# Unscaled token rows stored by tile for the experts' gathers, the factor in a column behind them, and x loaded by tiles

## The chip, the cores and the metric

The kernel runs as one program on one core of one Trainium2 chip. The metric is the device time of one execution, in microseconds; smaller is better. Inside the core five engines work side by side, each through its own list of instructions in a fixed order: PE (TensorE, matrix products), DVE (VectorE) and ACT (ScalarE) for elementwise work, POOL (GpSimd) for small work and for issuing some transfers, and SP (SyncE), which here only issues transfers. An instruction that waits for another engine or for a transfer holds up all that stands behind it in its own list.

## The reference, cut to what matters

The model has two layers on 512 tokens of width 1024: a mixer (differential attention in layer 0, sparse attention in layer 1), and after each a mixture of experts. For the experts each token is divided by its root mean square, scaled and shifted by two vectors, and sent to two of 32 experts:

```
h   = rmsnorm(x) * (1 + scale) + shift          # x: 512 x 1024
top = two best of 32 experts per token (4 groups of 8)
y_e = (silu(h @ w_gate[e]) * (h @ w_up[e])) @ w_down[e]      # hidden width 256
x   = x + gate2 * sum over the two experts of weight * y_e
```

## The kernel before

**Residual.** The residual rows live in the tile `xs` (128 partitions x 4 token tiles x 1024). It is filled from the input by one transfer of 2 MB that ACT issues (L644) while layer 0's output projection runs. That projection (`out_proj`) works on token tiles 0 and 1 first, then 2 and 3; the results of each half are multiplied into `otmp` (L607) and added to `xs` (L608) on DVE. Then PE transposes `xs` for the router (L700), token tile by token tile.

**Routing.** For each token tile `route` computes the router's logits (transposes L700, copies on ACT L702, products L705), then the factor 1/rms, called `r4` in the code and `r_h` in the rows (ACT square with sum L326, DVE L327, POOL power L328). The helper `row` multiplies the token rows by that factor on DVE (L728) and POOL stores the result in the DRAM buffer `xr_d` (L729). A table of slots says which tokens go to which expert, 64 slots for each expert. After the table there is a branch for experts with more tokens than slots (L949); it is not taken here.

**Experts.** The 32 experts run as 16 pairs, 128 slots a pair, numbered 0 to 15 below. For each pair, in the function `pair`: POOL gathers 128 rows of `xr_d` (L838) into one of two buffers `xg`; PE transposes them in two lots of four (L852) and ACT (L857) and DVE (L859) copy the transposes to `xT`, scaling and shifting them; PE multiplies with the gate and up weights (L864, 32 products of 128x512 to a pair of 64-column halves); ACT forms `sl` (L867), DVE forms `ac` (L869); PE transposes `ac` (L873), and a copy to `aTm` follows. That copy is made by the helper `copy_any`, which takes ACT and DVE in turn: even pairs have it on ACT (L394), odd pairs on DVE (L395). DVE makes the one-hot matrix `st` (L881), PE multiplies with the down weights (L887, first half `b_sc`, second half `b_mm`, 8 products each), and each half passes through `y` (DVE, L890), `yh` (ACT, L370) and `yl` (DVE, L371).

The function `add` of a pair brings its result back to the token rows: 8 times two products (L898 and L899 on PE) and one addition into `xs` (L900 on DVE). It is called inside the next pair, between `aTm` and `st` in program order. For PE it is work that needs nothing of the pair whose `ac` and `aTm` are under way.

**Order.** A scheduler puts every engine's instructions in a fixed order when the program is built, from the dependences and from its own estimate of times; the kernel is written in the plain order above. The same scheduler orders the changed kernel anew, with other results. Weights stream through SP in pieces of 512 KB ahead of the pairs that need them.

Of the kernel before, what the change touches and what calls it, by code (L numbers as in the profile page):

```python
# [11 lines left out]
F32 = mybir.dt.float32  # L12
# [4 lines left out]
AF = mybir.ActivationFunctionType  # L17
OP = mybir.AluOpType
# [4 lines left out]
P = 128  # L23
S = 512
NT = S // P
D = 1024
# [55 lines left out]
def tile_kernel(ctx, tc, x, c, positions, ada_w, ada_b, norm_g, final_g, diff_w_in, diff_w_out,  # L82
# [3 lines left out]
    nc = tc.nc  # L86
    mm = nc.tensor.matmul
    x_d = x.rearrange("b s d -> (b s) d")
    out_d = out.rearrange("b s d -> (b s) d")

    dram = ctx.enter_context(tc.tile_pool(name="dram", bufs=1, space=DRAM))
# [6 lines left out]
    def bank(tag):  # L98
        return ps.tile([P, 512], F32, name="b_" + tag, tag=tag, bufs={"mm": 4, "tr": 2, "sc": 2}[tag])
# [35 lines left out]
    def slot(i, shape, dtype=F32):  # L135

        return rp.tile(shape, dtype, name=f"slot{i}", tag=f"slot{i}", bufs=1)
# [4 lines left out]
    ident = cst.tile([P, P], F32, name="ident")  # L142
# [125 lines left out]
    with tc.tile_pool(name="rope", bufs=1) as rpool:  # L268
# [3 lines left out]
        kk = rpool.tile([P, NT, 8], F32, name="kk")  # L272
# [50 lines left out]
    def rms(pool, xt, rcol, tag=("junk", 1)):  # L323

        junk = pool.tile([P, D], BF16, name="junk", tag=tag[0], bufs=tag[1])
        nc.scalar.activation(junk, xt, AF.Square, accum_out=rcol)  # L326
        nc.vector.tensor_scalar(rcol, rcol, 1.0 / D, EPS, op0=OP.mult, op1=OP.add)  # L327
        nc.gpsimd.tensor_tensor(rcol, rcol, mhalf[:, 0:1], op=OP.pow)  # L328
# [6 lines left out]
    def by_k(row):  # L335

        return row.rearrange("t (p k) -> t k p", k=KC)
# [31 lines left out]
    def stack_k(src, h_out, l_out):  # L369
        nc.scalar.activation(h_out, src, AF.Copy)  # L370
        nc.vector.tensor_tensor(l_out, src, h_out.bitcast(F32), op=OP.subtract)  # L371
# [19 lines left out]
    def copy_any(dst, src):  # L391
        ev[0] += 1
        if ev[0] % 2:
            return nc.scalar.activation(dst, src, AF.Copy)  # L394
        return nc.vector.tensor_copy(dst, src)  # L395

    class Experts:
# [47 lines left out]
        def gu(self, e, k):  # L445
            return self.have["g", e, k // 4][:, :, k % 4, :]

        def dn(self, e, k, z):
            return self.have["d", e, 0][:, k, z * 512:(z + 1) * 512]
# [191 lines left out]
    main.close()  # L641
    xpool = ctx.enter_context(tc.tile_pool(name="xs", bufs=1))
    xs = xpool.tile([P, NT, D], F32, name="xs")
    nc.scalar.dma_start(xs, x_d.rearrange("(t p) d -> p t d", p=P))  # L644


    def tap(name, xs):
        if name in TAPS:
            nc.sync.dma_start(TAPS[name].rearrange("(t p) d -> p t d", p=P), xs)

    xr_d = dram.tile([S, D], F32, name="xr_d")

    def open_moe(l):
        st = ExitStack()
# [31 lines left out]
    def open_moe2(l, g):  # L686
        g.st2 = ExitStack()
        g.mq = g.st2.enter_context(tc.tile_pool(name=f"moeb{l}", bufs=1, side="right"))
        g.xg = [g.mq.tile([P, D], F32, name=f"xg{i}") for i in range(2)]

    def apx(t, dims, off=0):
        return bass.AP(tensor=t.tensor, offset=t.offset + off, ap=[t.ap[0]] + dims)
# [1 line left out]
    def logits(g, lb, t):  # L694

        xk = by_k(g.xs[:, t, :])
        for q in range(2):
            b = bank("tr")
            for kk in range(4):
                nc.tensor.transpose(b[:, kk * P:(kk + 1) * P], xk[:, 4 * q + kk, :], ident)  # L700
            ht = g.mp.tile([P, 512], F32, name="ht", tag="xT", bufs=2)
            nc.scalar.activation(ht, b, AF.Copy)  # L702
            for kk in range(4):
                k = 4 * q + kk
                mm(lb[:, t * NL:(t + 1) * NL], ht[:, kk * P:(kk + 1) * P], g.wr[:, k, :],  # L705
                   start=(k == 0), stop=(k == KC - 1), skip_group_check=True)

    def route(l, g):
        mp, mq, xs = g.mp, g.mq, g.xs
        fold_router(g)  # L710
        lb = bank("sc")
        r4 = mp.tile([P, NT], F32, name="r_h")
# [10 lines left out]
        oh2 = oh.rearrange("p (c t) e -> p c (t e)", c=2)  # L723
        M = mq.tile([P, NT, NE], BF16, name="M")

        def row(t):
            xr = g.xg[t] if t < 2 else mq.tile([P, D], F32, name="xr", tag="yh" if t == 2 else "yl", bufs=1)
            nc.vector.tensor_scalar(xr, xs[:, t, :], r4[:, t:t + 1], None, op0=OP.mult)  # L728
            g.stored = nc.gpsimd.dma_start(xr_d[t * P:(t + 1) * P, :], xr)  # L729

        for t in range(NT):
            logits(g, lb, t)
            rms(mp, xs[:, t, :], r4[:, t:t + 1])
            if t < NT - 1:
                row(t)
        for t in range(NT):
            nc.vector.scalar_tensor_tensor(lg[:, t], lb[:, t * NL:(t + 1) * NL], r4[:, t:t + 1], g.rb, op0=OP.mult, op1=OP.add)
            nc.vector.max(g8[:, t], lg[:, t, 0:8])
# [5 lines left out]
        for t in range(NT):  # L744
# [3 lines left out]
                                       op0=OP.mult, op1=OP.add)  # L748
        nc.vector.tensor_tensor(oh, dup(g.iota[:, 0:NE], 2 * NT),
                                eid.rearrange("p c t -> p (c t)")[:, :, None].to_broadcast([P, 2 * NT, NE]), op=OP.is_equal)  # L750
        nc.vector.tensor_tensor(M.rearrange("p t e -> p (t e)"), oh2[:, 0], oh2[:, 1], op=OP.add)
        row(NT - 1)

        rk = bank("sc")
        mm(rk[:, 0:P], upper, M.rearrange("p t e -> p (t e)"), start=True, stop=False, skip_group_check=True)
# [86 lines left out]
    def pair(g, q, tab, gu, dn, xg, between=None):  # L842


        mp = g.mq
        toks, tokf, wts = tab
        xT = g.mp.tile([P, KC, P], F32, name="xT", bufs=2)
        for z in range(2):
            b = bank("tr")
            for kk in range(4):  # L850
                k = 4 * z + kk
                nc.tensor.transpose(b[:, kk * P:(kk + 1) * P], by_k(xg)[:, k, :], ident)  # L852
            for kk in range(4):
                k = 4 * z + kk
                src = b[:, kk * P:(kk + 1) * P]
                if kk % 2:
                    nc.scalar.activation(xT[:, k, :], src, AF.Identity, scale=g.Ac[:, k:k + 1], bias=g.shc[:, k:k + 1])  # L857
                else:
                    nc.vector.tensor_scalar(xT[:, k, :], src, g.Ac[:, k:k + 1], g.shc[:, k:k + 1],  # L859
                                            op0=OP.mult, op1=OP.add)  # L860
        hb = bank("mm")
        for k in range(KC):
            for a in range(2):
                mm(hb[64 * a:64 * a + 64, :].rearrange("p (z n) -> p z n", z=2), xT[:, k, 64 * a:64 * a + 64], gu(a, k),  # L864
                   start=(k == 0), stop=(k == KC - 1), skip_group_check=True)
        sl = mp.tile([P, HID], F32, name="sl", bufs=2)
        nc.scalar.activation(sl, hb[:, 0:HID], AF.Silu)  # L867
        ac = mp.tile([P, HID], F32, name="ac", bufs=2)
        nc.vector.tensor_tensor(ac.rearrange("p (k t) -> p t k", k=2), hb[:, HID:512].rearrange("p (t k) -> p t k", k=2),  # L869
                                sl.rearrange("p (t k) -> p t k", k=2), op=OP.mult)  # L870
        b = bank("tr")
        for k in range(2):
            nc.tensor.transpose(b[:, k * P:(k + 1) * P], ac[:, k * P:(k + 1) * P], ident)  # L873
        aT = mp.tile([P, 2, P], F32, name="aTm", bufs=2)
        copy_any(aT.rearrange("p k t -> p (k t)"), b[:, 0:HID])
        if between is not None:
            between()
        yh = mp.tile([P, D], F32R, name="yh", bufs=1)
        yl = mp.tile([P, D], F32R, name="yl", bufs=1)
        st = mp.tile([P, S], F32R, name="st", bufs=2)  # L880
        nc.vector.tensor_scalar(st, g.iota, tokf[:, q:q + 1], None, op0=OP.is_equal)  # L881
        for z in range(2):
            yb = bank("mm" if z else "sc")
            zz = slice(z * 512, (z + 1) * 512)
            for k in range(2):
                for a in range(2):
                    mm(yb[64 * a:64 * a + 64, :], aT[:, k, 64 * a:64 * a + 64], dn(a, k, z), start=(k == 0), stop=(k == 1),  # L887
                       skip_group_check=True)
            y = mp.tile([P, 512], F32, name="y", bufs=2)
            nc.vector.scalar_tensor_tensor(y, yb, wts[:, q:q + 1], g.g2[:, zz], op0=OP.mult, op1=OP.mult)  # L890
            stack_k(y, yh[:, zz], yl[:, zz])

        def add():
            for t in range(NT):
                for z in range(2):
                    zz = slice(z * 512, (z + 1) * 512)
                    b = bank("mm" if z else "sc")
                    mm(b, st[:, t * P:(t + 1) * P], yh[:, zz], start=True, stop=False)  # L898
                    mm(b, st[:, t * P:(t + 1) * P], yl[:, zz], start=False, stop=True)  # L899
                    nc.vector.tensor_tensor(g.xs[:, t, zz], g.xs[:, t, zz], b, op=OP.add)  # L900

        return add
# [57 lines left out]
    g = open_moe(0)  # L960
# [3 lines left out]
    wout_stack.close()  # L964
    tap("x0a", g.xs)
    open_moe2(0, g)
    experts(0, g, ew, route(0, g))
    tap("x0m", g.xs)

# [8 lines left out]
    xr = [slot(i, [P, 2, D]) for i in range(2)]  # L978
# [103 lines left out]
    b = bank("tr")  # L1082
# [44 lines left out]
    b = bank("tr")  # L1127
# [4 lines left out]
    b = bank("mm")  # L1132
# [12 lines left out]
    b = bank("mm")  # L1145
# [104 lines left out]
    g = open_moe(1)  # L1250
# [5 lines left out]
    wout_stack.close()  # L1256
    tap("x1a", g.xs)
    open_moe2(1, g)
    experts(1, g, ew, route(1, g))
    tap("x1m", g.xs)  # L1260
    fg = bcp.tile([P, D], F32, name="bc")
# [33 lines left out]
```

## Time and profile before

| | us |
|---|---|
| median of 3 runs | 1410.16 (1410.09 to 1411.47) |
| the profiled execution, its own time | 1411.33 |
| its span, first to last instruction | 1409.5 |
| PE busy | 1282.6 (91%) |
| DVE busy | 786.7 (56%) |
| ACT busy | 514.6 (37%) |
| POOL busy | 169.4 (12%) |

The span is what the trace shows; the own time of that execution is 1.8 us longer, and the median of the timed runs lies 1.2 us under that own time. Busy shares are means over the whole span. The mean clock granted to PE over the span is 0.956 of full speed.

### The profile page before, as it was taken

To read this page: it belongs to the slowest core of one execution; us is meant where nothing else is said; L and a number is where in the kernel's file an instruction comes from. 1 tells how busy PE (TensorE), PEld (TensorE's weight loads), DVE (VectorE), ACT (ScalarE), POOL (GpSimd) and SP (SyncE) were. 2 spreads that over 40 slices of the span, in tenths; PEclk is the share of its full clock that TensorE was granted. 3 is DMA by queue.
4 is the path that set the end of the run, shared out by engine and by line. 5 is a ranking of instruction groups with operands and counts; after the bars stand their busy time and mean duration, and the time that the engine had idled before them with its cause. 6 is when DMAs were issued, how large, how long until landed. Compare 5 with 4: busy or idle time off the path is not lost. (4 is left out here: it accounts for less than half of the span.)

```text
span 1409.5 us, 18225 instructions
## 1 busy us (share of the span) xinstructions
PE 1282.6 (91%) x6431; PEld 759.2 (54%) x6431; DVE 786.7 (56%) x1791; ACT 514.6 (37%) x1188; POOL 169.4 (12%) x298
## 2 busy tenths in 40 slices
PE   4899999978879999999799799999999699999995
PEld 0687668567733544444588555555568434444342
DVE  2454755485635666655554365656635446666555
ACT  2454544454322222111454444656644212222212
POOL 0021020211110000000042111111220200000000
PEclk7899999999989999999899899999999699999998
DMA  7633764585579999992332174510153599999931
GB/s 253 219 104 112 244 209 150 180 289 193 185 244 363 390 405 408 379 350 95 109 120 90 60 255 147 148 51 1 54 161 120 182 362 369 407 408 409 364 141 60
DMA packets 104493, 309.81 MB, mean 220 GB/s; under 512 B 13776, under 2 KB 27568, under 8 KB 104388
## 3 DMA queue, kind: packets, MB, share of 16 engines
q1 hardware_dynamic: 93920, 288.59, 57.4%
q0 software_dynamic: 6240, 12.95, 2.7%
q10 hardware_dynamic: 4228, 6.96, 1.6%
q8 instruction: 55, 0.90, 0.3%
q14 instruction: 50, 0.41, 0.1%
HBM read 310.51 MB, written 6.33 MB: 225 GB/s over the span
## 5 line engine op out<-in xcount | busy, mean ns | idle before, releaser
L864 PE MATMUL b_mm<-slot,xT 128*64 128x512 f32 x640 | 199.3, 604 | 0.0
L864 PE MATMUL b_mm<-ring,xT 128*64 128x512 f32 x384 | 135.9, 597 | 0.0
L362 PE MATMUL b_mm<-wh,h_hi 128*128 128x512 f32 (+1 forms) x320 | 116.1, 394 | 8.3 <-ACT wh L358 6.6
L363 PE MATMUL b_mm<-wl,h_hi 128*128 128x512 f32 (+1 forms) x320 | 122.5, 391 | 0.7 <-DVE wl L359 0.7
L364 PE MATMUL b_mm<-wh,h_lo 128*128 128x512 f32 (+1 forms) x320 | 120.6, 387 | 0.0
L857 ACT ACTIVATE xT<-b_tr,col_sh,col_A 128x128 f32<-128x128 f32 x128 | 56.5, 455 | 148.2 <-DVE xT L859 146.9
L864 PEld LDWEIGHTS b_mm<-slot,xT 128*64 128x64 f32 x640 | 58.1, 139 | 87.3 <-issue 80.6
L900 DVE TENSOR_TENSOR xs<-xs,b_sc 128x512 f32<-128x512 f32 x128 | 83.4, 683 | 23.0 <-PE b_sc L899 23.0
L900 DVE TENSOR_TENSOR xs<-xs,b_mm 128x512 f32<-128x512 f32 x128 | 82.1, 682 | 19.3 <-PE b_mm L899 19.3
L189 PE MATMUL b_mm<-ring,csil 128*32 128x512 f32 x384 | 76.0, 657 | 11.8 <-DMA ring<-in_ada_w_dram 6.9
L838 POOL DMA_INDIRECT xg<-xr_d,toks x32 | 32.0, 1000 | 432.3 <-PE b_tr L852 411.8
L867 ACT ACTIVATE sl<-b_mm 128x256 f32<-128x256 f32 x32 | 12.3, 385 | 186.9 <-PE b_mm L864 186.9
L869 DVE TENSOR_TENSOR ac<-b_mm,sl 128x256 f32<-128x256 f32 x32 | 19.7, 617 | 107.7 <-ACT sl L867 107.7
L359 DVE TENSOR_TENSOR wl<-ring,wh 128x512 fp32r<-128x512 f32 (+1 forms) x80 | 53.1, 672 | 35.9 <-ACT wh L358 34.3
L1216 ACT ACTIVATE pT<-b_tr 128x512 f32<-128x512 f32 x80 | 47.4, 597 | 65.2 <-PE b_tr L1214 64.6
L362 PEld LDWEIGHTS b_mm<-wh,h_hi 128*128 128x128 f32 x320 | 60.3, 191 | 19.9 <-ACT wh L358 7.3
L386 DVE TENSOR_REDUCE nm<-b_sc 128x1 f32<-128x128 f32 (+3 forms) x116 | 54.3, 482 | 27.5 <-PE b_sc L381 26.8
L370 ACT ACTIVATE yh<-y 128x512 fp32r<-128x512 f32 x64 | 39.9, 632 | 79.5 <-DVE y L890 79.5
L363 PEld LDWEIGHTS b_mm<-wl,h_hi 128*128 128x128 f32 x320 | 61.0, 191 | 12.4 <-DVE wl L359 1.4
L358 ACT ACTIVATE wh<-ring 128x512 fp32r<-128x512 f32 (+1 forms) x80 | 48.4, 614 | 50.7 <-PE b_mm L364 36.2
L364 PEld LDWEIGHTS b_mm<-wh,h_lo 128*128 128x128 f32 x320 | 60.8, 190 | 11.1
L864 PEld LDWEIGHTS b_mm<-ring,xT 128*64 128x64 f32 x384 | 39.9, 137 | 49.4 <-issue 46.8
(329 smaller groups left out, 2678.5 us busy)
## 6 DMA issues: line engine op xcount, KB each, us to landing
ring<-in_ada_w_dram SPq DMA_DIRECT2D x96, 512.0 KB, 4.9
slot<-in_moe_w_gate_dram SPq DMA_DIRECT2D x80, 512.0 KB, 8.4
slot<-in_moe_w_up_dram SPq DMA_DIRECT2D x80, 512.0 KB, 4.4
dn<-in_moe_w_down_dram SPq DMA_DIRECT2D x80, 512.0 KB, 8.0
slot<-in_moe_w_down_dram SPq DMA_DIRECT2D x48, 512.0 KB, 8.6
ring<-in_moe_w_gate_dram SPq DMA_DIRECT2D x48, 512.0 KB, 10.1
ring<-in_moe_w_up_dram SPq DMA_DIRECT2D x48, 512.0 KB, 4.4
ring<-in_diff_w_in_dram SPq DMA_DIRECT2D x24, 512.0 KB, 4.8
```

What stands on the lines that cost most here:

```text
L189: mm(acc[32 * g:32 * g + 32, :], lhsT, w[:, c0:c0 + 512], start=(k == 0), stop=(k == KC - 1), skip_group_check=True)
L358: nc.scalar.activation(wh[:, :n], w[:, k, :], AF.Copy)
L359: nc.vector.tensor_tensor(wl[:, :n], w[:, k, :], wh[:, :n].bitcast(F32), op=OP.subtract)
L362: mm(accs[t][:, :n], hi[:, k, tt], wh[:, :n], start=(k == 0), stop=False)
L363: mm(accs[t][:, :n], hi[:, k, tt], wl[:, :n], start=False, stop=False)
L364: mm(accs[t][:, :n], lo[:, k, tt], wh[:, :n], start=False, stop=(k == KC - 1))
L370: nc.scalar.activation(h_out, src, AF.Copy)
L386: nc.vector.tensor_reduce(nm, b[:, :n], axis=AX.X, op=OP.max, negate=True)
L857: nc.scalar.activation(xT[:, k, :], src, AF.Identity, scale=g.Ac[:, k:k + 1], bias=g.shc[:, k:k + 1])
L864: mm(hb[64 * a:64 * a + 64, :].rearrange("p (z n) -> p z n", z=2), xT[:, k, 64 * a:64 * a + 64], gu(a, k), start=(k == 0), stop=(k == KC - ...
L900: nc.vector.tensor_tensor(g.xs[:, t, zz], g.xs[:, t, zz], b, op=OP.add)
L1216: nc.scalar.activation(pT, b, AF.Copy)
```

## The change

The residual `xs` is loaded in four transfers of 512 KB, one for each token tile, in place of one. `xr_d` and the two `xg` buffers get one column more (1025). The rows of `xs` are stored in `xr_d` as they are, right behind each tile's logits, and DVE's four multiplications by the factor per layer (L728) are gone. The factors of all 512 tokens go into the last column by one more POOL transfer of 512 single numbers; the event `g.stored`, after which a stretch of weight transfers may start, is now that transfer. POOL clears both `xg` buffers once a layer. In `pair` a new ACT instruction multiplies the gathered rows by their last column into a new tile `xn` (one buffer), and the transposes read `xn`. The tile `y` has one buffer in place of two.

```diff
-    nc.scalar.dma_start(xs, x_d.rearrange("(t p) d -> p t d", p=P))
+    for t in range(NT):
+        nc.scalar.dma_start(xs[:, t, :], x_d[t * P:(t + 1) * P, :])
...
-    xr_d = dram.tile([S, D], F32, name="xr_d")
+    xr_d = dram.tile([S, D + 1], F32, name="xr_d")
...
-        g.xg = [g.mq.tile([P, D], F32, name=f"xg{i}") for i in range(2)]
+        g.xg = [g.mq.tile([P, D + 1], F32, name=f"xg{i}") for i in range(2)]
+        for xg in g.xg:
+            nc.gpsimd.memset(xg, 0.0)
...
-        def row(t):
-            xr = g.xg[t] if t < 2 else mq.tile([P, D], F32, name="xr", tag="yh" if t == 2 else "yl", bufs=1)
-            nc.vector.tensor_scalar(xr, xs[:, t, :], r4[:, t:t + 1], None, op0=OP.mult)
-            g.stored = nc.gpsimd.dma_start(xr_d[t * P:(t + 1) * P, :], xr)
...
             logits(g, lb, t)
+            nc.gpsimd.dma_start(xr_d[t * P:(t + 1) * P, 0:D], xs[:, t, :])
             rms(mp, xs[:, t, :], r4[:, t:t + 1])
-            if t < NT - 1:
-                row(t)
+        with nc.allow_non_contiguous_dma("512 factors"):
+            g.stored = nc.gpsimd.dma_start(xr_d[:, D:D + 1].rearrange("(t p) o -> p (t o)", p=P), r4)
...
-        row(NT - 1)
...
+        xn = mp.tile([P, D], F32, name="xn", bufs=1)
+        nc.scalar.activation(xn, xg[:, 0:D], AF.Copy, scale=xg[:, D:D + 1])
...
-                nc.tensor.transpose(b[:, kk * P:(kk + 1) * P], by_k(xg)[:, k, :], ident)
+                nc.tensor.transpose(b[:, kk * P:(kk + 1) * P], by_k(xn)[:, k, :], ident)
...
-            y = mp.tile([P, 512], F32, name="y", bufs=2)
+            y = mp.tile([P, 512], F32, name="y", bufs=1)
```

From L847 on, lines of `pair` and `add` stand one lower in the changed kernel (`ac` is L870 there, the additions L901, the down products L888, the copies to `aTm` still L394 and L395).

The order of instructions changes too. First DVE in pair 3 of layer 0, before: `ac`, the additions of pair 2's result, the copy to `aTm`, `st`, and the start of the copies to `xT`.

```order
L869 TENSOR_TENSOR ac<-b_mm,sl 128x128x2
L900 TENSOR_TENSOR xs<-xs,b_sc 128x512
L900 TENSOR_TENSOR xs<-xs,b_mm 128x512
L900 TENSOR_TENSOR xs<-xs,b_sc 128x512
L900 TENSOR_TENSOR xs<-xs,b_mm 128x512 x2
L395 COPY aTm<-b_tr 128x256
L900 TENSOR_TENSOR xs<-xs,b_mm 128x512
L859 TENSOR_SCALAR xT<-b_tr,col_A_2994,col_sh_2992 128x128
L900 TENSOR_TENSOR xs<-xs,b_sc 128x512 x2
L881 TENSOR_SCALAR st<-iota_t,tv 128x512
```

The same stretch of DVE in the changed kernel:

```order
L901 TENSOR_TENSOR xs<-xs,b_sc 128x512 x2
L901 TENSOR_TENSOR xs<-xs,b_mm 128x512
L870 TENSOR_TENSOR ac<-b_mm,sl 128x128x2
L901 TENSOR_TENSOR xs<-xs,b_mm 128x512 x2
L901 TENSOR_TENSOR xs<-xs,b_sc 128x512 x2
L901 TENSOR_TENSOR xs<-xs,b_mm 128x512
L882 TENSOR_SCALAR st<-iota_t,tv 128x512
L395 COPY aTm<-b_tr 128x256
L860 TENSOR_SCALAR xT<-b_tr,col_A_2997,col_sh_2995 128x128 x2
```

Three additions moved ahead of `ac`, and the last three with `st` moved ahead of the copy. The copy to `aTm` now stands last, behind `ac`, five additions and `st`. Odd pairs 3, 5, 7, 9 and 11 have this order in both layers, pair 13 in layer 0 too.

PE around the same place before: the end of pair 3's gate and up products, the products of the previous pair's `add`, and the transposes of `ac`.

```order
L864 MATMUL b_mm<-slot_6541,xT 64x512
L898 MATMUL b_sc<-yh,st 128x512 x2
L899 MATMUL b_sc<-yl,st 128x512
L898 MATMUL b_mm<-yh,st 128x512
L899 MATMUL b_mm<-yl,st 128x512
L899 MATMUL b_sc<-yl,st 128x512
L898 MATMUL b_mm<-yh,st 128x512
L899 MATMUL b_mm<-yl,st 128x512
L898 MATMUL b_mm<-yh,st 128x512
L899 MATMUL b_mm<-yl,st 128x512
L873 MATMUL b_tr<-ident,ac 128x128 x2
```

The same place on PE in the changed kernel, up to the down products:

```order
L865 MATMUL b_mm<-slot_6577,xT 64x512
L900 MATMUL b_mm<-yl,st 128x512 x2
L899 MATMUL b_mm<-yh,st 128x512
L900 MATMUL b_mm<-yl,st 128x512
L899 MATMUL b_sc<-yh,st 128x512
L900 MATMUL b_sc<-yl,st 128x512
L899 MATMUL b_sc<-yh,st 128x512
L900 MATMUL b_sc<-yl,st 128x512
L899 MATMUL b_mm<-yh,st 128x512
L900 MATMUL b_mm<-yl,st 128x512
L874 MATMUL b_tr<-ident,ac 128x128 x2
L853 MATMUL b_tr<-ident,xn 128x128 x4
```

Before, all 16 products of `add` come behind the last gate and up product: ten ahead of the transposes of `ac`, and six behind them (the last four behind the transposes of `xg`), just before the down products. Now six of them stand among the gate and up products and ten behind, all ahead of the transposes of `ac`; nothing but four transposes stands between those and the down products. In both layers pairs 3 to 9 had the order shown for before or one close to it. Counted over all pairs, the products of `add` stand like this on PE. Before: pairs 1 and 2 have eight among the gate and up products and eight behind them, pairs 3 to 9 have all behind, pairs 11 to 15 have all 16 early among them and none behind. Changed: pairs 1, 2, 4, 6, 8, 10 and 12 have ten among them (in three groups, as pairs 1 and 2 before) and six behind; pairs 3, 5, 7, 9 and 11 six and ten; pairs 13 to 15 have seven and nine, ten and six, ten and six in layer 0, and 14 and two, 14 and two, 16 and none in layer 1. On DVE the copy to `aTm` of pair 1 stood behind `ac`, four additions and `st`, and stands behind `ac`, three additions and `st` now.

POOL while routing layer 0, in the changed kernel (before: three powers, three stores, a power, a store, and no clearing):

```order
L732 DMA xr_d<-xs 128x1024
L328 TENSOR_TENSOR r_h<-r_h,mhalf 128x1
L732 DMA xr_d<-xs 128x1024
L328 TENSOR_TENSOR r_h<-r_h,mhalf 128x1
L732 DMA xr_d<-xs 128x1024
L328 TENSOR_TENSOR r_h<-r_h,mhalf 128x1
L693 MEMSET xg_3361 128x1025
L693 MEMSET xg_3362 128x1025
L732 DMA xr_d<-xs 128x1024
L328 TENSOR_TENSOR r_h<-r_h,mhalf 128x1
L735 DMA xr_d<-r_h 128x4x1
```

The transfer of the factors is the last of the five writes to `xr_d` that each gather has to wait for.

## Rows read from the trace of the kernel before

**Rows 1.** Page: busy time of each engine, share of the span, instructions.

```profile
PE 1282.6 (91%) x6431; PEld 759.2 (54%) x6431; DVE 786.7 (56%) x1791; ACT 514.6 (37%) x1188; POOL 169.4 (12%) x298
```

**Rows 2.** Chain that ended last, layer 1's experts, PE's down products: start, us, what.

```profile
1129.32 1.94 PE b_sc L887 x8
1131.25 1.72 PE b_mm L887 x8
...
1148.29 3.26 PE b_sc L887 x8
1151.55 2.09 PE b_mm L887 x8
...
1166.96 1.94 PE b_mm L887 x8
...
1278.57 1.94 PE b_mm L887 x8
...
1295.68 1.94 PE b_sc L887 x8
...
1387.68 1.99 PE b_sc L887 x8
```

**Rows 3.** Timeline, pair 1 of layer 1: start, us, instruction, [idle before <-releaser].

```profile
1142.93 0.59 PE L864 MATMUL b_mm<-ring,xT 128*64 128x512 f32 x1
...
1144.59 0.62 DVE L869 TENSOR_TENSOR ac<-b_mm,sl 128x256 f32<-128x256 f32 x1
...
1145.04 0.68 DVE L900 TENSOR_TENSOR xs<-xs,b_mm 128x512 f32<-128x512 f32 x1
...
1145.64 0.60 PE L852 MATMUL b_tr<-ident,xg 128*128 128x128 f32 x4
...
1147.42 0.48 DVE L881 TENSOR_SCALAR st<-iota_t,tv 128x512 fp32r<-128x512 f32 x1
1147.82 0.42 DVE L395 COPY aTm<-b_tr 128x256 f32<-128x256 f32 x1
...
1148.29 3.26 PE L887 MATMUL b_sc<-dn,aTm 128*64 128x512 f32 x8 [2.05 <-DVE aTm L395]
```

**Rows 4.** Windows, layer 1: stretch, length, five engines busy, PEclk, DMA share, GB/s.

```profile
1146.00:1148.00 2.00, 0.24 (x3) 0.05 (x1) 2.00 (x5) 0.00 (x0) 0.00 (x0) 1.00 1.03 412
...
1149.00:1152.00 3.00, 3.00 (x8) 0.74 (x8) 0.82 (x2) 0.57 (x2) 0.00 (x0) 0.50 1.02 408
```

**Rows 5.** Timeline, layer 1, pair 13: PE behind the last gate product.

```profile
1350.18 0.44 PE L873 MATMUL b_tr<-ident,ac 128*128 128x128 f32 x2 [1.11 <-DVE ac L869]
```

**Rows 6.** Timeline, layer 0: down products of pairs 0, 1 and 15.

```profile
409.21 1.94 PE L887 MATMUL b_sc<-slot,aTm 128*64 128x512 f32 x8
...
428.23 3.40 PE L887 MATMUL b_sc<-dn,aTm 128*64 128x512 f32 x8 [2.05 <-DVE aTm L395]
...
667.61 1.94 PE L887 MATMUL b_sc<-slot,aTm 128*64 128x512 f32 x8 [0.52 <-DVE aTm L395]
```

**Rows 7.** Timeline, layer 0's output projection: the load of x and its readers.

```profile
330.16 0.39 ACTq L644 DMA_DIRECT2D xs<-in_x_dram  x1
...
344.24 0.69 DVE L608 TENSOR_TENSOR xs<-xs,otmp 128x512 f32<-128x512 f32 x1 [5.33 <-DMA xs<-in_x_dram]
...
346.23 1.94 PE L700 MATMUL b_tr<-ident,xs 128*128 128x128 f32 x8 [5.24 <-DVE xs L608]
```

**Rows 8.** Windows around that wait (columns as in group 4).

```profile
345.00:350.00 5.00, 3.77 (x13) 3.42 (x14) 4.80 (x9) 2.52 (x5) 0.11 (x1) 0.50 0.67 216
350.00:355.00 5.00, 5.00 (x26) 4.18 (x26) 2.17 (x4) 3.28 (x6) 1.02 (x2) 1.00 0.21 38
```

**Rows 9.** Timeline, routing of layer 1 up to pair 0.

```profile
1098.94 0.58 POOL L729 DMA_DIRECT2D xr_d<-xr  x1 [1.09 <-DVE xr L728]
...
1101.81 0.76 DVE L737 SCALAR_TENSOR_TENSOR lg<-b_sc,r_h,rb 128x40 f32<-128x40 f32 x4 [3.17 <-PE b_sc L705]
...
1109.72 1.11 POOL L838 DMA_INDIRECT xg<-xr_d,toks  x1 [2.98 <-DVE toks L825]
...
1117.07 1.95 PE L852 MATMUL b_tr<-ident,xg 128*128 128x128 f32 x8 [3.62 <-DVEq L949]
```

**Rows 10.** Transfers of the whole execution: the router table's 1024 runs of 16 bytes.

```profile
wr<-in_moe_w_group_dram POOLq DMA_DIRECT2D x2, 16.0 KB, 6.9
```

**Rows 11.** Groups by line and form, ACT.

```profile
L326 ACT ACTIVATE junk<-xs 128x1024 bf16<-128x1024 f32 x12 | 12.7, 1056 | 14.2 <-DVE xs L608 9.5 <-DVE xs L900 3.5 <-DVE r_h L327 1.0
```

## The prediction, made before the changed kernel ran

> **What bounds the kernel now.** I read the page first: PE is busy for 1282.6 of 1409.5 us [rows 1], so a change pays only where PE waits, or where PE's own work is stretched. So I followed PE through the chain of waits in the expert stage and then looked at the timeline wherever PE stood still. The reader is to see three places.
>
> First, the pace of the expert pairs. From the down products of pair 0 to those of pair 15 layer 1 takes 1387.68 - 1129.32 = 258.36 us, layer 0 667.61 - 409.21 = 258.40 [rows 2, 6]. The pace is uneven: steps 1 and 2 take 18.97 and 18.67, steps 3 to 9 (1278.57 - 1166.96) / 7 = 15.94, step 10 takes 17.11, steps 11 to 15 (1387.68 - 1295.68) / 5 = 18.40 [rows 2].
>
> Second, why steps 1 and 2 are slow. In pair 1 the last gate product ends at 1143.52. PE goes on with eight products of `add`, the transposes of `ac` and four of `xg` until 1146.24, and then stands still for 2.05 us for the copy to `aTm`, which waits on DVE behind `ac`, four additions of about 0.6 (1145.04 to 1147.42) and `st` [rows 3]. The granted clock, 1.00 in the two us before, is 0.50 (1.2 GHz in place of 2.4) once the down products begin [rows 4]; they take 3.26 + 2.09 where pair 0 has 1.94 + 1.72, so 1.69 more [rows 2]. Layer 0 has the same wait of 2.05 and then 3.40 for the first half [rows 6]. Taking wait and clock away, step 1 is 18.97 - 2.05 = 16.92 and step 2 is 18.67 - 1.69 = 16.98: with gate products and `add` interleaved as in pairs 1 and 2, a pair costs 16.95 when nobody waits. The waits of the late pairs (1.11 before the transposes of `ac` in pair 13, about 0.5 for the copy [rows 5, 6]) leave the clock alone: the down products behind them take 1.99 [rows 2].
>
> Third, layer 0's output projection: the 2 MB of x are asked for at 330.16, DVE's first addition waits until 344.24, and PE stands still for 5.24 us [rows 7]. Afterwards the clock is 0.50 until about 350 [rows 8].
>
> **The change, part by part.**
>
> *Load of x by tiles.* The one load takes 14.1 us. If four pieces come in the order asked for, the first is there after about a quarter of it (333.7, an estimate), tile 1 by 337.2, and the first addition no longer waits. Gain: the 5.24 us, and the half clock, in which PE's 3.77 busy us did about 1.9 us of work less than at full clock [rows 7, 8]: 7.1. If all four land together, 0. I take -7, as two tiles are enough for the first half of the projection.
>
> *DVE's scalings gone.* They are worth nothing: behind them DVE waits 3.17 us for the router's products on PE [rows 9]. If that cover were gone, each would count about as much as ACT's pass over the same shape, 1.06 [rows 11].
>
> *The new order of the experts.* This is the large term. Even pairs 2 to 12 now have the interleaved form of pairs 1 and 2, with ACT's copy and no long queue before it: 16.95, six times. That is 1.0 more than the 15.94 that steps 4, 6 and 8 had. Odd pairs 3 to 11 have DVE's copy behind `ac`, five additions and `st`. Against pair 1 of rows 3 that is one addition more (+0.60) while PE has two products more to do (-0.48, at 1.94 for eight): a wait of 2.17 us. Their form has one break less in the gate products, so I take 16.8 for the work: 18.95 each. Pair 1 has three additions behind `ac` where it had four, and none just before it (-1.2), but two products fewer behind the last gate product (+0.48): wait 1.3, step 18.3. Pairs 13 to 15 mix the forms; from the products behind the last gate product I take 54.1 for the three (18.2, 17.6 and 18.3 in layer 1; 19.1, 16.95 and 18.0 in layer 0), against 55.2 before. Per layer: 18.3 + 101.7 + 94.8 + 54.1 = 268.9, against 258.4: +10.5, twice +21.0. Bounds: if the interleaved form costs only the 15.94 of steps 3 to 9, the sum is 18.3 + 6 x 15.94 + 5 x 18.1 + 54.1 = 258.5, no change; if every odd pair waits 2.8 (one addition late), +13.7 a layer.
>
> *The clock behind those waits.* Ten waits of about 2.2 us, a little longer than the two of 2.05 that halved the clock both times, each worth 1.69 if it does so again: between 0 and +16.9. Two of two speaks for nearly always; what PE did just before differs a little, so I take three in four: +12.7.
>
> *`xn` on ACT.* One pass of 128x1024 costs about 1.06 [rows 11]. In the new order it stands between the two `yh` of a pair, almost a pair ahead of the transposes that read it. It pushes the second `yh` back by about half a us, and with one buffer `y` the second half waits for the first `yl`. What hides both: four transposes and eight gate products (in the trace 16 halves) stand ahead of the first product of `add`, more ahead of the second half's. Cost 0. If that cover fails by half a us, it is 15 x 0.5 in each layer, +15. In pair 0 `xn` must run between gather and transposes; there PE waits for the branch until 1117.07, 7.35 us after the gather was issued at 1109.72 [rows 9], so 0 to +1.1 a layer: I take +0.5 for both.
>
> *Stores, column, clearing.* The stores leave without waiting for the factor. The last write is now the column, issued about when the last store was (1098.94), and the gather goes at 1109.72 [rows 9]: 10.8 us for it. The nearest row, 1024 runs of 16 bytes, lands in 6.9 [rows 10], so it is hidden: 0, at most +3 a layer if it queues behind a store. The Trainium skill, page "DMA: Bandwidth & Descriptors", section "Rules for kernel authors", says that a strided last dimension becomes one descriptor for each element, and advises a contiguous one. By that rule the column is 512 descriptors; half as many as the runs of rows 10, so the sum would stay as it is unless single numbers cost more than twice as much as 16-byte runs. POOL's clearing falls in its idle time.
>
> *Sum.* 1411.33 - 7 + 21.0 + 12.7 + 0.5 = 1438.5 as this execution's own time; the median lies 1.2 under it: 1437.
>
> **Rivals.**
>
> - *The waits come, the clock holds.* For it: waits of 1.1 leave the clock alone. Against: both waits of 2.05 did not. 1411.3 - 7 + 21 - 1.2 = 1424 (with half the losses 1431). 0.2.
> - *More than I count.* Every wait halves the clock, the column or `xn` makes pair 0 late, or the chain `y`, `xn`, `yh`, `yl` holds up `add`: 1442 to 1455. For it: the new ACT instruction stands in that chain and `y` has lost a buffer. 0.14.
> - *Faster.* One mechanism: the 1.0 us that pairs 1 and 2 cost beyond pairs 3 to 9 is not the interleaving but the start of the stage, and even pairs run at 15.94. Then the pairs cancel out, and without clock losses the load of x decides: 1411.3 - 7 - 1.2 = 1403. It decides once the even pairs fall under about 16.3 and the clock holds. Against: both layers show the same 16.9, and pair 2 has no wait. 0.08.
> - *No change.* That mechanism, and the four pieces of x land together, so that the wait stays: 1410. 0.03.
>
> **How the numbers follow.** Forecast 1437 with 0.55 (1431 to 1441); the others as given. Slower 0.55 + 0.2 + 0.14 = 0.89, faster 0.08, same 0.03, where 0.2% (2.8 us) is about what can be told from no change in this kernel. For 8 in 10 the range leaves out the faster and equal cases and the outer end of the dearer one: 1419 to 1447.
>
> **What would show it.** PE's first down product of odd pairs 3 to 11 should be released by DVE's copy after about 2.2 us, with a granted clock of 0.5 behind most of them; even pairs should show no such wait and steps near 17. Around 340 the wait for x should be gone with the half clock after it. The ACT row of `xn` should take about 1.06, with PE not waiting for it except in pair 0, and the gather should be released by the table and not by the column. I am wrong if the copy runs soon after `ac` on DVE, if the clock holds at 1.00 through the waits, or if PE waits for `yl` in the products of `add`.

## The result, and the profile after

| | before | changed |
|---|---|---|
| median, us | 1410.82 | 1446.01 (4 runs, 1443.66 to 1449.95) |
| profiled execution: own time, us | 1411.33 | 1443.66 |
| its span, us | 1409.5 | 1441.9 |

The change makes the kernel slower: ratio 1.0239, 95% interval 1.022 to 1.0258 (the two medians of the table divide to 1.0249, inside it). The forecast was 1437, range 1419 to 1447.

The page of the changed kernel, busy time of each engine, beside [rows 1]: PE works 27 us longer for the same 6431 instructions, so part of the loss is work at a lower rate and not waiting.

```profile
PE 1309.7 (91%) x6431; PEld 752.2 (52%) x6431; DVE 783.5 (54%) x1783; ACT 546.5 (38%) x1220; POOL 176.1 (12%) x304
```

The chain that ended last, down products in layer 1, beside [rows 2] (start, us, what):

```profile
1141.59 1.94 PE b_sc L888 x8
...
1159.87 1.94 PE b_sc L888 x8
...
1176.84 1.94 PE b_sc L888 x8
...
1195.62 3.49 PE b_sc L888 x8
...
1214.27 1.94 PE b_sc L888 x8
...
1420.04 1.94 PE b_sc L888 x8
```

The steps are the differences of the starts: 18.28, 16.97, 18.78, 18.65 and so on. The 15 steps take 278.45 us where [rows 2] gave 258.36. Step 2 shows the interleaved form with nothing in its way, step 3 the wait of an odd pair, step 4 the slow clock behind it (3.49 for a half that takes 1.94).

What makes the interleaved form dearer where nobody waits can be read from the starts in the timeline. In pair 2 of layer 1 `add` breaks into the gate and up products three times; counted from the start of each group to the start of what follows, the gate and up products take 7.47 us and `add` 4.43. In pair 5 of e6 below, with the gate and up products unbroken by `add`, they take 7.02 and 4.07, and the transposes 0.36 less. That is the 1.16 between their steps, 16.97 and 15.81.

The timeline of pair 3 in layer 1 of the changed kernel, beside [rows 3]:

```profile
1189.16 1.08 PE L865 MATMUL b_mm<-slot,xT 128*64 128x512 f32 x4
...
1190.71 0.69 DVE L901 TENSOR_TENSOR xs<-xs,b_mm 128x512 f32<-128x512 f32 x1 [3.77 <-PE b_mm L900]
1191.32 0.62 DVE L870 TENSOR_TENSOR ac<-b_mm,sl 128x256 f32<-128x256 f32 x1
1191.77 1.27 DVE L901 TENSOR_TENSOR xs<-xs,b_mm 128x512 f32<-128x512 f32 x2
...
1192.79 0.61 PE L853 MATMUL b_tr<-ident,xn 128*128 128x128 f32 x4
1192.96 1.27 DVE L901 TENSOR_TENSOR xs<-xs,b_sc 128x512 f32<-128x512 f32 x2
1194.16 0.67 DVE L901 TENSOR_TENSOR xs<-xs,b_mm 128x512 f32<-128x512 f32 x1
1194.76 0.47 DVE L882 TENSOR_SCALAR st<-iota_t,tv 128x512 fp32r<-128x512 f32 x1
1195.14 0.42 DVE L395 COPY aTm<-b_tr 128x256 f32<-128x256 f32 x1
1195.62 3.49 PE L888 MATMUL b_sc<-slot,aTm 128*64 128x512 f32 x8 [2.22 <-DVE aTm L395]
```

PE is through with its last transposes at 1193.40. DVE, the whole time busy, goes through five additions and `st` before it comes to the copy. The transposes of `ac`, which the copy needs, had been over for more than 2 us (they end at 1192.96).

Windows of the changed kernel (columns as in group 4), the first two around that wait, the third behind the same wait in pair 3 of layer 0:

```profile
1193.00:1195.00 2.00, 0.40 (x4) 0.21 (x2) 2.00 (x5) 0.00 (x0) 0.00 (x0) 1.00 0.98 379
1196.00:1199.00 3.00, 3.00 (x10) 0.84 (x8) 0.41 (x1) 0.89 (x2) 0.00 (x0) 0.50 0.97 311
...
455.60:459.50 3.90, 3.90 (x18) 1.38 (x19) 1.81 (x4) 1.54 (x3) 0.00 (x0) 1.00 0.96 290
```

The clock went to half in one case and stayed full in the other, after the same wait of 2.22. Of the 11 waits between 2.21 and 2.42 in both layers, eight were followed by down products at the lower clock.

Timeline of layer 0 in the changed kernel, beside [rows 7]: the four loads of x, DVE's first addition, PE's first transposes of `xs`. Neither waits now, and the window behind them has the full clock where [rows 8] had half (the last number but two).

```profile
329.28 0.34 ACTq L645 DMA_DIRECT2D xs<-in_x_dram  x1
329.66 2.31 ACTq L645 DMA_DIRECT2D xs<-in_x_dram  x3
...
337.58 0.68 DVE L608 TENSOR_TENSOR xs<-xs,otmp 128x512 f32<-128x512 f32 x1
...
339.98 1.05 PE L704 MATMUL b_tr<-ident,xs 128*128 128x128 f32 x8
```

```profile
345.00:350.00 5.00, 5.00 (x31) 4.41 (x30) 2.26 (x5) 2.78 (x6) 0.58 (x1) 1.00 1.15 371
```

Then layer 0's way from the slots to pair 0. Before, the last store, the slots and the first gather:

```profile
380.37 0.57 POOL L729 DMA_DIRECT2D xr_d<-xr  x1 [1.08 <-DVE xr L728]
...
388.17 0.17 DVE L825 TENSOR_SCALAR toks<-tv 128x16 int32<-128x16 f32 x1
...
390.10 1.23 POOL L838 DMA_INDIRECT xg<-xr_d,toks  x1 [4.44 <-DVE wt L789]
```

Changed: the slots, the first gather, and, behind the branch, ACT's table load, `xn` and the transposes:

```profile
379.48 0.17 DVE L824 TENSOR_SCALAR toks<-tv 128x16 int32<-128x16 f32 x1
...
379.94 1.15 POOL L837 DMA_INDIRECT xg<-xr_d,toks  x1 [2.98 <-DVE toks L824]
...
386.78 1.28 ACT L847 ACT_TABLE_LOAD   x1 [6.40 <-PEq L950]
...
388.07 1.15 ACT L847 ACTIVATE xn<-xg 128x1024 f32<-128x1024 f32 x1
...
389.27 1.97 PE L853 MATMUL b_tr<-ident,xn 128*128 128x128 f32 x8 [5.61 <-ACT xn L847]
```

The 32.4 us between the two spans, cut at the first gather and at the down products of pairs 0 and 15 of each layer:

| stretch | changed minus before, us |
|---|---|
| up to layer 0's first gather (390.10 to 379.94) | -10.2 |
| gather to pair 0's down products, layer 0 and 1 | +2.5, +2.8 |
| the 15 steps of layer 0 (258.40 to 275.83) | +17.4 |
| the 15 steps of layer 1 (258.36 to 278.45) | +20.1 |
| all the rest | -0.2 |

### The profile page after: what moved, and what is told of

It reads as the page before. It is cut to its first block, busy times and chain, and to the rows that moved or that the text cites. A ratio compares the mean times of both kernels' runs of the same rounds, so it can differ in the third digit from the quotient of the medians.

```text
span 1441.9 us, 18347 instructions
## 1 busy us (share of the span) xinstructions
PE 1309.7 (91%) x6431; PEld 752.2 (52%) x6431; DVE 783.5 (54%) x1783; ACT 546.5 (38%) x1220; POOL 176.1 (12%) x304
## 5 line engine op out<-in xcount | busy, mean ns | idle before, releaser
L865 PE MATMUL b_mm<-slot,xT 128*64 128x512 f32 x640 | 204.6, 613 | 0.0
L865 PE MATMUL b_mm<-ring,xT 128*64 128x512 f32 x384 | 139.1, 603 | 0.0
L901 DVE TENSOR_TENSOR xs<-xs,b_mm 128x512 f32<-128x512 f32 x128 | 82.6, 680 | 77.6 <-PE b_mm L900 77.6
L901 DVE TENSOR_TENSOR xs<-xs,b_sc 128x512 f32<-128x512 f32 x128 | 82.2, 681 | 59.4 <-PE b_sc L900 59.4
L865 PEld LDWEIGHTS b_mm<-slot,xT 128*64 128x64 f32 x640 | 53.1, 139 | 79.8 <-issue 66.6
L860 DVE TENSOR_SCALAR xT<-b_tr,col_A,col_sh 128x128 f32<-128x128 f32 x128 | 51.9, 407 | 30.1 <-ACT xT L858 24.3
L371 DVE TENSOR_TENSOR yl<-y,yh 128x512 fp32r<-128x512 f32 x64 | 44.3, 692 | 38.5 <-ACT yh L370 37.3
L888 PE MATMUL b_sc<-dn,aTm 128*64 128x512 f32 x160 | 44.7, 685 | 19.1 <-DVE aTm L395 18.8
```

## The experiments

The question was whether the loss lies in the order, and what makes the order, or in the new work (`xn`, the column, the gather) or in the smaller buffer itself. All medians stand beside runs of the kernel before on the same chip; ratios are to those, with their 95% interval.

**e1_x_tiles: the load of x by tiles alone.**

```diff
-    nc.scalar.dma_start(xs, x_d.rearrange("(t p) d -> p t d", p=P))
+    for t in range(NT):
+        nc.scalar.dma_start(xs[:, t, :], x_d[t * P:(t + 1) * P, :])
```

> The kernel before with the load of x by tiles alone. The order of the expert pairs stays, but for pairs 10 and 11 of layer 0. My theory: the wait for x (5.24 us) and the half clock behind it go, 7 us, and the up to 3 us more that the changed kernel gained by the first gather come from the load too: 1400.5 to 1404. Rival: the 3 us more came from DVE's four scalings that are gone, then 1403.5 to 1404.5. If the load is hidden anyway: 1411.

Measured 1407.95 (1403.78 to 1412.96) against 1411.72, ratio 0.9969 (0.9956 to 0.9983). From the load's issue to the first gather the profile takes 53.3 us (329.80 to 383.08) where the kernel before takes 59.9 (330.16 to 390.10): the 6.7 of the load are there, the up to 3 more that my theory put down to it are not. In the profiled execution (1412.11, the second slowest of the ten) the gain was given back in layer 1's mixer. The edit does not touch that stage's code, but the scheduler ordered it anew: between about 690 and 930 us the instructions of PE and DVE stand in another order. Windows of e1, then of the kernel before:

```profile
700.00:760.00 60.00, 58.16 (x305) 49.51 (x304) 27.94 (x66) 29.60 (x62) 20.46 (x76) 0.97 0.34 104
760.00:820.00 60.00, 52.12 (x290) 35.81 (x288) 24.51 (x64) 22.79 (x46) 9.75 (x22) 0.83 0.33 104
```

```profile
700.00:760.00 60.00, 57.41 (x312) 49.08 (x311) 31.25 (x70) 32.54 (x66) 20.18 (x76) 1.00 0.34 102
760.00:820.00 60.00, 51.33 (x301) 36.88 (x299) 24.10 (x61) 24.06 (x47) 10.02 (x23) 0.89 0.29 95
```

The clock is 0.03 and 0.06 lower there. Instruction for instruction, e1's lead over the kernel before falls from 6.0 to 2.6 us across these windows, and the rest is lost by 930 us, at a clock of 1.00 in both. The median kept 3.8 of the gain. My band was missed. Why this stage lost time, and whether its new order is the reason, is open.

**e2_one_y: one buffer for `y`, nothing else.**

```diff
-            y = mp.tile([P, 512], F32, name="y", bufs=2)
+            y = mp.tile([P, 512], F32, name="y", bufs=1)
```

> The kernel before with one buffer for y in place of two, nothing else. Its order then has the interleaved form in layer 1 in pairs 1 to 13 (odd pairs with five products of add among the gate and up products and eleven behind, the copy to aTm behind ac, five additions and st), in layer 0 only up to pair 6; pairs 8 and 9 of layer 0 keep the old order in spite of the one buffer. My theory (the order, and it comes from y's buffer): layer 1 about +18, layer 0 about +7, 1432 to 1438; odd pairs wait about 1.9 to 2.2 for DVE's copy; pairs 8 and 9 of layer 0 still take about 15.9. Rival (xn on ACT or the gathered column makes the pairs slow): 1411, no wait of that kind. Rival (the single buffer itself delays yl): pairs 8 and 9 of layer 0 over 17 too.

Measured 1437.75 (1432.34 to 1438.68) against 1411.72, ratio 1.0172 (1.0147 to 1.0196), inside my band. Timeline of e2, PE's down products in layer 0 for pairs 6 and 7 (pair 7 has the old order), then in layer 1 for pairs 2 and 3 (new order):

```profile
518.00 1.94 PE L887 MATMUL b_mm<-slot,aTm 128*64 128x512 f32 x8
...
533.85 1.94 PE L887 MATMUL b_mm<-dn,aTm 128*64 128x512 f32 x8
...
1174.70 1.94 PE L887 MATMUL b_sc<-dn,aTm 128*64 128x512 f32 x8
...
1193.26 3.41 PE L887 MATMUL b_sc<-slot,aTm 128*64 128x512 f32 x8 [1.95 <-DVE aTm L395]
```

With the same single buffer, the step is 15.85 in the old order and 18.56 in the new. This small edit alone brings the new order (in layer 0 only up to pair 6) and most of the loss, 26 of 35 us; the buffer as such costs nothing where the order stays.

**e3_xn_in_place: the whole change, `xn` made in place, two buffers for `y`.**

```diff
-        xn = mp.tile([P, D], F32, name="xn", bufs=1)
-        nc.scalar.activation(xn, xg[:, 0:D], AF.Copy, scale=xg[:, D:D + 1])
+        nc.scalar.activation(xg[:, 0:D], xg[:, 0:D], AF.Copy, scale=xg[:, D:D + 1])
...
-            y = mp.tile([P, 512], F32, name="y", bufs=1)
+            y = mp.tile([P, 512], F32, name="y", bufs=2)
```

The transposes read `xg` again.

> The whole change, but the gathered rows are scaled in place in xg, without the tile xn, and with the memory that this leaves y has two buffers again. Its order is near that of before in both layers. My theory (y's buffer sets the order, the order makes the loss): the pairs cost what they did before or up to 4 us less, x gains 7 to 10, pair 0 loses 2.2 in each layer: 1400 to 1406, faster than before. Rival (xn's ACT pass, the column or the gather is the loss): 1430 or more.

Measured 1408.06 (1405.98 to 1410.5) against 1411.72, ratio 0.9973 (0.996 to 0.9986): faster than before, 2 us above my band. Scaling on ACT, the column and the wider rows are all still in it, so none of them is the loss of 35 us. Two buffers for `y` give the old order back, but for some pairs of layer 1, where steps 11 and 12 took 20.4 and 20.3 (1.69 of step 12 is down products at the lower clock).

**e4_copy_on_act: the changed kernel, all copies to `aTm` on ACT.**

```diff
-        copy_any(aT.rearrange("p k t -> p (k t)"), b[:, 0:HID])
+        nc.scalar.activation(aT.rearrange("p k t -> p (k t)"), b[:, 0:HID], AF.Copy)
```

> The changed kernel with all 32 copies to aTm on ACT, one buffer for y kept. The order then has all products of add behind the gate and up products in pairs 3 to 7 and early ones from pair 9 on. My theory (the loss is DVE's copy behind the additions, and the clock behind that wait): no wait of about 2.2 for the copy, no half clock behind it, 1400 to 1410. Rival (one buffer for y, or xn between the two yh, holds up the products of add whatever the order): PE waits for yh or yl in most pairs, 1425 or more.

Measured 1415.35 (1414.09 to 1417.37) against 1411.72, ratio 1.0023 (1.0013 to 1.0032): 31 us of the loss are gone, 5 more than I allowed are left. No wait of 2.2 and no down products at the lower clock remain. Waits of PE for `ac` in e4 (in total, times, longest):

```profile
PE b_tr L874 <- DVE ac L870: 16.5, 16, 1.2
```

Steps 3 to 7 take 15.8; from step 9 on, where the scheduler puts nearly all products of `add` early, they take 18.5 to 20.05, more than the 18.40 of the kernel before. That is again the order more than the rival: most of these pairs have 14 products of `add` behind the first two gate products and two more later, and take 18.97; the kernel before has that order once, in pair 11, and took 18.90 for it. The rival wanted PE to wait for `yh` or `yl` in most pairs; it waits for `yh` once in each layer (0.75, pair 9), and once for an addition (1.15, pair 12).

**e5_before_adds_last: the kernel before, with the products of `add` behind the gate and up products.** The edit constrains only the order of issue on PE; no buffer and no arithmetic changes.

```diff
-                mm(hb[64 * a:64 * a + 64, :].rearrange("p (z n) -> p z n", z=2), xT[:, k, 64 * a:64 * a + 64], gu(a, k),
+                last = mm(hb[64 * a:64 * a + 64, :].rearrange("p (z n) -> p z n", z=2), xT[:, k, 64 * a:64 * a + 64], gu(a, k),
...
-            between()
+            with tc.issue_after(last.ins):
+                between()
```

> The kernel before with one edit: on PE the products of add may only be issued behind the pair's last gate and up product, so that all pairs have the order of pairs 3 to 9. My theory (the order sets the pace): 15 steps of about 15.95 in each layer in place of 258.4 in all, 239, and so 1373 to 1380, if the weights keep up (6 MB a pair at the 408 GB/s of the trace is 15.4). Rival (pairs 10 to 15 are slow because their weights come late, and the order only fills the time): PE then waits for weights in the gate and up products, 1400 to 1410.

Measured 1372.5 (1371.37 to 1373.66) against 1410.87, ratio 0.9723 (0.9707 to 0.9739). The chain of e5, the halves issued first of the down products of pairs 0, 1, 2 and 15 in layer 1:

```profile
1109.99 1.94 PE b_sc L888 x8
...
1125.90 1.87 PE b_mm L888 x8
...
1142.18 1.87 PE b_mm L888 x8
...
1348.10 1.94 PE b_mm L888 x8
```

238.11 us for the 15 steps, 258.36 before. Pairs 1 and 2 now take 15.9 and 16.3, so their 16.95 was the interleaving and not the start of the stage. Pairs 11 to 15 take 15.9 in place of 18.4, and PE does not wait for weights.

**e6_after_adds_last: the changed kernel with the same edit of the order** (the diff is that of e5).

> The changed kernel, with one buffer for y, with xn and the column, and that same single edit of the order. My theory: the whole loss of the change was its order, so with the same order as e5 it takes 4 to 6 less than e5 (x by tiles and the route -7 to -9.5, pair 0 +2.2 in each layer), 1367 to 1376. Rival (one buffer for y and xn between the two yh cost PE something in every pair): 10 or more above e5.

Measured 1367.4 (1366.09 to 1368.47) against 1410.87, ratio 0.9689 (0.9673 to 0.9706), 5.1 under e5. Down products of pairs 0, 1 and 15 in layer 1 of e6, in its timeline:

```profile
1103.44 1.94 PE L889 MATMUL b_sc<-slot,aTm 128*64 128x512 f32 x8
...
1119.23 1.94 PE L889 MATMUL b_mm<-dn,aTm 128*64 128x512 f32 x8
...
1340.81 1.94 PE L889 MATMUL b_mm<-slot,aTm 128*64 128x512 f32 x8 [0.23 <-DVE aTm L395]
```

237.37 us for 15 steps. With the order held fixed by the same constraint in both, the change makes the kernel 5 us faster; with the scheduler's order it makes it 35 us slower.

**e7_x_adds_last: e5 with the load of x by tiles**, and **e8_x_adds_last_copy_act: e7 with all copies on ACT** (diffs as in e1, e4 and e5).

> e5 with the load of x by tiles. 4 to 7 under e5: 1366 to 1376. If the load is worth as little as in e1: 3 to 4 under e5.

> e7 with all copies to aTm on ACT. The odd pairs' wait of 0.51 for DVE's copy goes, 15.8 a step: 4 to 5 under e7, 1362 to 1372, the fastest of the four. If the clock or the weights set the pace: as e7.

Measured 1366.05 (1365.4 to 1368.48), ratio 0.9683 (0.9667 to 0.9699), and 1363.04 (1362.13 to 1365.49), ratio 0.9659 (0.9643 to 0.9675), against 1410.87. In e7 the load of x is worth 6.5. In e8 the waits for DVE's copy are gone and the 15 steps take 235.38. e8 beats both kernels, by 47.8 and some 83 us.

**e9_after_adds_last_xn_dve: e6 with the rows scaled on DVE**, and **e10_after_adds_last_xn_dve_copy_act: e9 with all copies on ACT.**

```diff
-        nc.scalar.activation(xn, xg[:, 0:D], AF.Copy, scale=xg[:, D:D + 1])
+        nc.vector.tensor_scalar(xn, xg[:, 0:D], xg[:, D:D + 1], None, op0=OP.mult)
```

> e6 with the gathered rows scaled on DVE in place of ACT. In the changed kernel the way from the first gather to the first down product is 2.1 to 2.5 us longer in each layer than before, and I put that down to ACT's table load (1.28) and its pass (1.15), both of which now stand between the branch and the transposes. If so, DVE's pass (about 0.75, no table load ahead of it) gives back 0.5 to 1.5 us of it in each layer; the steps of the pairs stay near 15.8: 1364 to 1367 against 1367 for e6. Rival (the gather or the column is late): the way stays 2.1 to 2.5 longer. Rival (DVE has no room for 16 passes more): steps of 16.3 and more, 1372 or later.

> e9 with all copies to aTm on ACT, so that each of the two engines has one of the two tasks. If the wait for DVE's copy or DVE's load matters: 1 to 4 under e9, 1361 to 1366; if neither does: as e9.

Measured 1369.28 (1367.69 to 1371.58), ratio 0.9707 (0.969 to 0.9724), and 1365.67 (1363.56 to 1368.48), ratio 0.9674 (0.9651 to 0.9696), against 1411.19. The steps stay at 15.8. Timeline of e9: layer 0, then layer 1.

```profile
385.38 1.28 ACT L858 ACT_TABLE_LOAD   x1 [5.97 <-ACTq L951]
386.60 0.75 DVE L847 TENSOR_SCALAR xn<-xg 128x1024 f32<-128x1024 f32 x1 [3.69 <-DVEq L951]
...
387.50 1.94 PE L853 MATMUL b_tr<-ident,xn 128*128 128x128 f32 x8 [4.80 <-DVE xn L847]
...
1080.38 1.12 POOL L837 DMA_INDIRECT xg<-xr_d,toks  x1 [2.97 <-DVE toks L824]
...
1090.25 0.75 DVE L847 TENSOR_SCALAR xn<-xg 128x1024 f32<-128x1024 f32 x1 [5.93 <-issue]
```

In layer 0 the table load now lies beside the branch and the way from the first gather to the first down product is 20.74, in e6 21.63. In layer 1 DVE's last event of the branch lies 7.2 us after the gather, but its pass starts 9.9 after it, for no wait that the profile names, and the way is 23.09 where e6 has 22.24. The same late start of DVE is in layer 1 of e8, which has no `xn`. In e10 the way is 20.68 and 20.08. So three of four layers speak for ACT's share; in all e9 is not faster than e6, and my band for e9 was missed by 2 us.

## Why the prediction was right, step by step

**The new order of the experts: right, and a little dearer than counted.** Forecast +21.0 without the clock. Measured: layer 1 20.1 less five losses of 1.69 is +11.6, layer 0 17.4 less three is +12.4, in all +24.0. Even pairs without a slow clock took 16.95 to 16.97 (forecast 16.95), odd pairs 18.77 to 18.79 (18.95), step 1 18.3 (18.3), the wait 2.22 (2.17). What was too small was the term of the last three pairs: 56.9 and 55.2 where I took 54.1 (before, they took 54.8, not 55.2). Pair 12 of layer 1, at 17.80 without the clock, was 0.85 dearer than its 16.95 too. e5 and e6 show that the order is the cause, e2 that the scheduler changes it when `y` has one buffer; e3, which changes more at once, agrees.

**The clock: right.** +12.7 for three in four of ten waits; it was eight of those ten, 8 x 1.69 = 13.5, and not behind the eleventh, of 2.42 in pair 13 of layer 0. That the wait's length decides it alone is refuted by the three that left the clock alone.

**The load of x: right.** Forecast -7. e1 shows -6.7 up to the first gather, e7 -6.5 in the median.

**DVE's scalings "worth nothing": wrong in layer 0.** The first gather came 10.2 us earlier, not 7. Of this 0.9 lies ahead of the load, which was issued at 329.28 and not at 330.16. From the load to that gather e3, which has the changed routing, shows 50.7 us where e1 has 53.3, so 2.6 belong to the routing (1.4 between e6 and e7). I looked only at layer 1 [rows 9], where the slots release the gather. In layer 0 before, the gather goes 1.8 us after the slots were ready and 9.7 after the last store was asked for, and these stores took 8.5 to 9.8 to land: it waited for the store, which had waited for the factor and the scaling. In e1 and e7 the same holds, 8.8 and 7.8 after the last store. The row of that gather above names DVE's `wt` as the releaser, which ended 0.24 before it. But in the kernel before and in e1, e2, e5, e7 and e8 that gather starts 0.96 or 0.97 us after the last store has landed (389.14 and 390.10 before), while `wt` ended 0.80 before it in e1 and only behind it in e5. So it was the store.

**Pair 0: too small.** Forecast +0.5 for both layers and at most +1.1 in each, measured +2.5 and +2.8. I had hidden `xn` behind the branch. But ACT loads a table ahead of it (1.28). Before, that load came 4.2 and 1.5 us after the first gather, while PE had to wait anyway. Now it stands with `xn` behind a wait that ends only when PE's own list comes out of the branch (386.78, [6.40 <-PEq L950]), 6.8 and 6.9 us after the gather; then comes the pass (1.15), and PE waits for both, 2.43 together. PE's first transposes start 2.4 and 2.1 later after the gather than before; the remaining 0.2 and 0.7 come behind them and stay open. e9 supports it in layer 0, e10 in both.

**`xn`, the single `y`, the column: hidden, as forecast.** e6 has them all at 15.8 a step. The column landed 7.6 and 8.7 us after its issue, and in both layers the slots released the first gather. The slack was thin in layer 0, though: with 0.96 from the landing to a gather, the column, landed at 378.40, would have let the gather go at 379.4, and it went at 379.94. In layer 0 of e6, e9 and e10 the column took 8.4 to 8.6 to land, and the gather goes 0.96 to 0.98 after its landing, some 0.2 to 0.5 us later than the slots alone would have it. Nor are these the times of the single numbers: the column landed 0.16 to 0.26 us behind the 512 KB store that POOL had issued about 1.5 us before it, in both layers of all six runs that have it. The Trainium skill, page "DMA: Bandwidth & Descriptors", section "Rules for kernel authors", warns of a strided last dimension. No run here shows what the column would take without a store ahead of it, so none tells what the single numbers cost; behind the store it was at most that quarter of a us.

**The rivals.** "Faster" rested on pairs 1 and 2 being slow because of the start of the stage: e5 refutes it. "The clock holds" is refuted by eight of eleven. "More than I count" is where the time came out, in its 1442 to 1455 and outside the 1431 to 1441 of the main case, but for part of its reasons only: `xn` made pair 0 late, and neither every wait halved the clock nor did `y` and `yl` hold up `add`. In the profiled execution, 5.2 above the 1438.5 of the sum, the terms missed by -3.2 (up to the first gather), +4.8 (pair 0), +3.0 (order), +0.8 (clock) and -0.2 (the rest). The other 3.8 of the 9 us by which the median missed are not in the sum: the changed kernel's profiled execution was the fastest of its four, 2.4 under their median, where I had taken the median to lie 1.2 under it.

What stays open: why equal waits leave the clock full in some pairs, why layer 1's mixer lost time in e1, and what the time of the first instruction behind the branch depends on.

## What to carry to other kernels

When a scheduler orders the program, compare the order of the instructions before the operations' costs: here one buffer less for a small tile, by itself, brought an order that cost about 26 us, while the work that the edit was about was hidden but for pair 0. Work without dependences on the critical pair (here `add`) is worth most exactly where the pair waits for another engine; placing it there by one constraint on issue order was worth 38 us, more than the whole change lost, in part because `add` no longer breaks into the gate and up products. And when a step is called hidden, look at every layer and at all that releases the reader: in one layer it was the slots, in the other a store.

## What the runs showed of the hardware that I had not expected

Waits of PE of the same length, 2.21 to 2.22 us, behind the same instructions, were followed by a granted clock of 0.50 in some pairs and of 1.00 in others (pairs 9 and 7 of layer 0, for instance). The three waits of 1.35 to 1.37 there were followed by 1.00; but in e3 a wait of 0.88 and one of 0.96 soon after it, in pair 1 of layer 0, were followed by 0.50, and nearly the same two in layer 1 (0.89 and 0.96) by 1.00. The 512 single numbers of the column landed 0.16 to 0.26 us behind a store of 512 KB issued before them on the same queue. A gather that had to wait for a store began 0.96 or 0.97 us after its landing in layer 0 of six runs. And the time from the first gather to DVE's first instruction behind the branch lay between 7.3 (e9, layer 0) and 9.9 us (e9, layer 1) for the same code.
